# Gate and up projections of 17 of 22 FFN tiles by seven block products, with the down projection between them

## The chip, the cores and the metric

The kernel runs on one core of a Trainium2 chip. The metric is the device time of one execution in microseconds (us), as the median of several runs; less is better.

## What is computed

A trunk of two layers over 512 tokens of width 1024, all in float32. Each layer is a mixer (retention in layer 0, differential attention in layer 1, each with a cross-attention into 256 memory tokens) and a dense feed-forward block. The change touches only the latter:

```python
FFN_DIM = -(-8 * D_MODEL // (3 * 256)) * 256        # 2816
x = x + jnp.concatenate([o_main, o_mem], axis=-1) @ w_out[layer]
h = rms_norm(x, ffn_norm_w[layer])
gu = h @ w_gate_up[layer]
x = x + (jax.nn.silu(gu[..., :FFN_DIM]) * gu[..., FFN_DIM:]) @ w_down[layer]
```

## The kernel before

Activations stand transposed: `xT[0..7]` are eight tiles of 128 features x 512 tokens. TensorE multiplies in float32r, and a float32 product is made of three matmuls: every operand is split into a high half (a rounded copy, made by ACT, `split_h`) and a low half (the rest, a subtraction on DVE, `split_l`), and `mm3` adds high x high, high x low and low x high into one accumulator.

Weights come in chunks of 128 x 1024 (`SPECS`, listed by `chunk_specs`). SP loads a chunk into one of three `wr` pages (`load_chunk`); `split_chunk` makes its halves in one of three `wh` and one of three `wl` pages. `chunk(...)` begins two chunks ahead of use. A page is written again only when its last reader is done, so a load waits for the split of the chunk three before it.

The FFN has 22 feature tiles of 128. `feat_tile` computes one output tile of 128 x 512 into one of eight accumulator banks `ps`, over 8 K tiles of the normed input `xw`. For each feature tile there is a gate and an up product, 2 x 8 x 3 = 48 matmuls of 512 columns. `swiglu` then multiplies both by the token norm `bc` on DVE (they are read from `ps` there), takes Silu on ACT, multiplies on POOL (on DVE for a subset's last tile) and splits the result into `ys` pages (tag `qk`). The 22 tiles go in three subsets (`SUBS`) of 8, 8 and 6; behind each, the down projection of that subset runs for the eight output tiles d, and `add_x` adds each to `xT` on DVE.

What sets the order is `Weave`, at build time. It follows a clock for every engine with costs written in `Engine`, and side streams (generators such as `swiglu` and `split_chunk`) are put into the engines' programs where that clock says that their inputs are ready; `pump` does so after each matmul. On the chip the order on each engine is then fixed: an instruction that waits holds all that stand behind it on its engine.

```python
        for i, (l_, r_) in enumerate(((aH, bH), (aH, bL), (aL, bH))):
            TE.matmul(out, lhsT=l_, rhs=r_, start=start and i == 0, stop=stop and i == 2)
```

Nearly all instructions carry line 251 in the profile (line 283 after the change), which is the helper in `Engine` that records them, so groups are told apart by their tiles.

## Time and profile before

| | us |
|---|---|
| median of 3 runs | 1180.24 |
| lowest and highest | 1178.43, 1182.14 |
| the profiled execution | 1181.2 |
| its span, first to last instruction | 1179.4 |
| PE busy in it | 1166.0 |
| DVE, ACT, POOL busy | 663.7, 480.7, 211.9 |
| one FFN (layer 0), in the span | 359.1 |

The span is read first against the busy time of each engine, then cut into stages. A row's duration runs from an instruction's start to its end; on PE, and by a little on DVE and ACT, neighbours overlap, so a rate is taken from starts.

### The profile page before, as it was taken

How to read it: one execution, taken by the hardware profiler on the slowest of the kernel's cores; microseconds unless marked ns; L12 is line 12 of the kernel's file. 1: busy time of each engine (PE TensorE's matmuls, PEld its weight loads, DVE VectorE, ACT ScalarE, POOL GpSimd, SP SyncE). 2: the span in 40 equal slices, each digit the busy share in tenths (PEclk: the TensorE clock that was granted, in tenths of full speed). 3: DMA queues.
4: the chain of work that ended last, by engine and by line, in shares of the span. 5: the costliest groups of instructions: out<-in, count | busy, mean ns of one | idle time of the engine just before them, and what ended most of it. 6: DMA issues, size and time to landing. Idle time of an engine off the chain costs nothing.

```text
span 1179.4 us, 14244 instructions
## 1 busy us (share of the span) xinstructions
PE 1166.0 (99%) x5546; PEld 966.2 (82%) x5546; DVE 663.7 (56%) x1049; ACT 480.7 (41%) x805; POOL 211.9 (18%) x143
## 2 busy tenths in 40 slices
PE   9999999999999999999999999999999999999998
PEld 7888888888888888888888777888888888888887
DVE  5679894455334443446556688866454344533442
ACT  6566763333213322235455566644332223322321
POOL 4020002211001100001553544224110000100010
PEclk9999999999999999999999999999999999999999
DMA  6432122322322222223422211113223223232322
GB/s 226 137 125 90 66 81 70 106 91 90 107 90 100 97 103 93 89 94 121 143 83 65 104 57 51 47 62 122 89 94 106 91 89 108 90 107 89 101 78 89
DMA packets 35058, 113.26 MB, mean 96 GB/s; under 512 B 4016, under 2 KB 4400, under 8 KB 34992
## 3 DMA queue, kind: packets, MB, share of 16 engines
q1 hardware_dynamic: 34848, 112.34, 27.7%
q8 instruction: 43, 0.70, 0.2%
q14 instruction: 23, 0.19, 0.0%
q10 hardware_dynamic: 144, 0.03, 0.0%
HBM read 110.26 MB, written 2.10 MB: 95 GB/s over the span
## 4 chain that ended last, share of the span: by engine, by line
PE 90%; DVE 5%; ACT 2%; POOL 1%; issue 1%; DMA 0%; SPq 0%; ACTq 0%; DVEq 0%; POOLq 0%
PE ps L251 90%; DVE sm L251 2%; DVE wk L251 2%; POOL tab L251 1%; ACT wk L251 1%; DVE mkL L251 1%; ACT wh L251 0%; DMA wr<-w_t 0%; DVE qk L251 0%; SPq L251 0%; ACT qk L251 0%; ACT L251 0%; ACT xw L251 0%; DVE qc L251 0%; ACT mkY L251 0%
## 5 line engine op out<-in xcount | busy, mean ns | idle before, releaser
L251 PE MATMUL ps<-xw,wh 128*128 128x512 f32 x1624 | 503.1, 390 | 0.0
L251 PEld LDWEIGHTS ps<-xw,wh 128*128 128x128 f32 x1624 | 304.3, 188 | 62.8
L251 ACT ACTIVATE wh<-wr 128x1024 fp32r<-128x1024 f32 (+2 forms) x200 | 204.4, 1024 | 359.9 <-PE ps L251 357.2
L251 DVE TENSOR_TENSOR wl<-wr,wh 128x1024 fp32r<-128x1024 f32 (+2 forms) x177 | 248.1, 1404 | 141.4 <-ACT wh L251 141.2
L251 PE MATMUL ps<-xw,wl 128*128 128x512 f32 x812 | 316.8, 390 | 0.0
L251 PE MATMUL ps<-qk,wh 128*128 128x512 f32 (+1 forms) x836 | 255.3, 386 | 0.0
L251 PEld LDWEIGHTS ps<-qk,wh 128*128 128x128 f32 x836 | 156.2, 188 | 31.8
L251 PEld LDWEIGHTS ps<-xw,wl 128*128 128x128 f32 x812 | 152.5, 188 | 31.0
L251 PE MATMUL ps<-qk,wl 128*128 128x512 f32 (+1 forms) x418 | 161.6, 387 | 0.0
L251 PE MATMUL ps<-wh,xw 128*128 128x512 f32 (+1 forms) x512 | 151.7, 374 | 2.9 <-DVE sm L251 2.9
L251 POOL TENSOR_TENSOR wk<-wk,wk 128x512 f32<-128x512 f32 x38 | 50.4, 1325 | 574.7 <-DVE wk L251 561.2
L251 DVE TENSOR_TENSOR wk<-ps,tab 128x512 f32<-128x512 f32 x94 | 64.4, 687 | 120.4 <-PE ps L251 114.6
L251 DVE TENSOR_TENSOR xT<-ps,xT 128x512 f32<-128x512 f32 (+1 forms) x65 | 44.3, 682 | 152.1 <-PE ps L251 152.0
L251 PEld LDWEIGHTS ps<-wh,xw 128*128 128x128 f32 x512 | 92.6, 191 | 19.2 <-DVE sm L251 3.6
L251 PE MATMUL ps<-wl,xw 128*128 128x512 f32 (+1 forms) x256 | 95.8, 374 | 0.4 <-DVE wl L251 0.4
L251 PEld LDWEIGHTS ps<-qk,wl 128*128 128x128 f32 x418 | 78.5, 188 | 15.6
L251 POOL TENSOR_TENSOR tab<-tab,tab 128x512 f32<-128x512 f32 x31 | 50.8, 1640 | 137.9 <-ACT tab L251 136.9
L251 ACT ACTIVATE qk<-wk 128x512 fp32r<-128x512 f32 (+2 forms) x74 | 41.8, 579 | 66.1 <-POOL wk L251 49.1
L251 POOL TENSOR_TENSOR wl<-wr,wh 128x1024 fp32r<-128x1024 f32 x23 | 55.5, 2417 | 71.8 <-ACT wh L251 67.1
L251 POOL TENSOR_TENSOR sm<-sm,mhalf 128x4 f32<-128x4 f32 (+1 forms) x36 | 44.3, 1238 | 129.0 <-DVE sm L251 128.7
L251 ACT ACTIVATE wk<-wk 128x512 f32<-128x512 f32 x50 | 31.6, 633 | 81.0 <-DVE wk L251 80.9
L251 PEld LDWEIGHTS ps<-wl,xw 128*128 128x128 f32 x256 | 48.8, 191 | 8.4 <-DVE wl L251 0.9
(129 smaller groups left out, 949.4 us busy)
## 6 DMA issues: line engine op xcount, KB each, us to landing
wr<-w_t SPq DMA_DIRECT2D x180, 512.0 KB, 3.5
wr<-w_t SPq DMA_DIRECT2D x16, 384.0 KB, 3.0
wr<-w_t SPq DMA_DIRECT2D x8, 256.0 KB, 5.1
xT<-x_t SPq DMA_DIRECT2D x8, 256.0 KB, 4.9
zo<-mem_t SPq DMA_DIRECT2D x8, 256.0 KB, 4.9
out_t<-xT SPq DMA_DIRECT2D x7, 256.0 KB, 2.0
tab<-dec_t SPq DMA_DIRECT2D x6, 256.0 KB, 3.8
tab<-ali_t SPq DMA_DIRECT2D x6, 256.0 KB, 3.9
```

What stands on the lines that cost most here:

```text
L251: return call(out, *args, **kw)
```

## The change

For the tiles of subset 0 (now 5) nothing changes. For the other 17, gate and up of one feature tile are one matrix product of 2 x 2 blocks: the weights are cut in rows gate and up and in K halves (`a11` gate and `a21` up of K tiles 0 to 3, `a12` and `a22` of K tiles 4 to 7), the input in K halves and in token halves of 256. By the scheme of Strassen in Winograd's form seven products of blocks do in place of eight, each over 4 K tiles, so 4 x 3 = 12 matmuls of 256 columns. For it:

- `token_halves` makes, once a layer while subset 0 runs, four sums of token blocks for each of 4 K tile pairs, split into halves (`tb`, in the pages `v` and `qc`).
- `weight_ops` makes for each tile the four weight sums `s1`, `s2`, `s3`, `s4` on DVE and splits seven operands of 128 x 512. The halves of one operand now share a page; `wh` and `wl` give six such pages, taken in turn, and at most six are live.
- `gate_up_pair` runs the seven products into three accumulators x, z and y. ACT copies x after each of three products and z after one; DVE sums the copies and the rest, applies the norm, and both products of swiglu stand on DVE and ACT.
- The down projection of a subset is cut into two pieces for each d (3 tiles and the rest). These pieces, loaded apart into `wk` pages, stand in the three gaps of each tile of the next subset (after `s1`, `s4`, `a12`); the last subset's run alone at the end.

Subsets are now 5, 6, 5 and 6. The diff's core:

```diff
-SUBS = ((0, 8), (8, 16), (16, 22))
+SUBS = ((0, 5), (5, 11), (11, 16), (16, 22))
+HT = T // 2
+KH = KT // 2
...
+                    if s == 0:
+                        specs.append((("gu", l, f, u), "w_gate_up", l, 0, KT, r(u * FFN + f * P, P)))
+                    else:
+                        both = r(f * P, P) + r(FFN + f * P, P)
+                        specs.append((("st", l, f, u), "w_gate_up", l, u * KH * P, KH, both))
...
-                specs.append((("down", l, s, d), "w_down", l, f0 * P, f1 - f0, r(d * P, P)))
+                for z, (a, b) in enumerate(pieces(s)):
+                    specs.append((("down", l, s, d, z), "w_down", l, (f0 + a) * P, b - a, r(d * P, P)))
...
+def pieces(s):
+    n = SUBS[s][1] - SUBS[s][0]
+    return (0, 3), (3, n)
+def gaps(s):
+    n = 3 * (SUBS[s][1] - SUBS[s][0])
+    skip = max(0, n - 2 * KT)
+    places = [[] for _ in range(n + 1)]
+    for i, z in enumerate((d, z) for d in range(KT) for z in range(2)):
+        places[min(i + skip, n)].append(z)
+    return places
...
+    def token_halves(layer, norm, tb):
+        while KT - 1 not in norm.xw:
+            yield 1.0
+        room = []
+        for tag, n, bufs in (("v", 3, 8), ("qc", KH, 2)):
+            for z in [page(tag, [P, n, HT], bufs, F32R) for _ in range(bufs)]:
+                room += [z[:, i, :] for i in range(n)]
+        a, b = slice(0, HT), slice(HT, T)
+        for j in range(KH):
+            x1, x2 = xT[j], xT[KH + j]
+            w1, w2 = col(norm.c + j), col(norm.c + KH + j)
+            yield from take(wk=3)
+            z = [wk([P, T])[:, s] for _ in range(3) for s in (a, b)]
+            A.activation(z[1], x1[:, b], AF.Copy, scale=w1)
+            V.tensor_tensor(z[0], x1[:, a], x1[:, b], op=ALU.subtract)
+            yield
+            V.scalar_tensor_tensor(z[2], x2[:, b], w2, z[1], op0=ALU.mult, op1=ALU.subtract)
+            V.scalar_tensor_tensor(z[3], x1[:, a], w1, z[2], op0=ALU.mult, op1=ALU.add)
+            V.scalar_tensor_tensor(z[4], x2[:, a], w2, z[3], op0=ALU.mult, op1=ALU.subtract)
+            parts = [(room.pop(), room.pop(), *src) for src in ((z[0], w1), (z[2],), (z[3], -1.0), (z[4], -1.0))]
+            yield
+            for part in parts:
+                yield from split(part)
+            give("wk", 3)
+            tb[j] = [part[:2] for part in parts]
...
+    def weight_ops(layer, order, ops, live):
...
+        def one(key, dH, dL, src, done):
+            W.cur = max(W.ready(src), W.ready(dH) - 0.2)
+            yield
+            split_h(dH, src)
+            yield
+            split_l(dH, dL, src)
+            n = dH.shape[1] // P
+            ops[key] = [[z[:, k * P:(k + 1) * P] for k in range(n)] for z in (dH, dL)]
+            done()
...
+        for key in order:
+            while live[0] >= 6:
+                yield 0.2
+            live[0] += 1
+            if key[0] == "down":
+                while key not in raws:
+                    yield 0.3
+                src = raws[key]
+                def done(key=key):
+                    del raws[key]
+                    give("wk", 1)
+            else:
+                _, _, fk, name = key
+                i1, i2 = [INDEX["st", layer, fk, u] for u in range(2)]
+                while i1 not in loaded or i2 not in loaded:
+                    yield 0.3
+                half = slice(0, T), slice(T, 2 * T)
+                a11, a21, a12, a22 = [loaded[i][0][:, s] for i in (i1, i2) for s in half]
+                if name == "a11":
+                    used1 = last(2, lambda i=i1: load_chunk(i + 3))
+                    used2 = last(3, lambda i=i2: load_chunk(i + 3))
+                    src, done = a11, used1
+                elif name == "s1":
+                    W.cur = max(W.ready(a11), W.ready(a22))
+                    yield
+                    yield from take(wk=2)
+                    s3, s1 = wk([P, T]), wk([P, T])
+                    V.tensor_tensor(s1, a21, a22, op=ALU.add)
+                    V.tensor_tensor(s3, a11, a21, op=ALU.add)
+                    src, done = s1, last(2, lambda: give("wk", 1))
+                    done1 = done
+                elif name == "s2":
+                    yield from take(wk=1)
+                    src = s2 = wk([P, T])
+                    V.tensor_tensor(s2, s1, a11, op=ALU.add)
+                    done1()
+                    used1()
+                    done = done2 = last(2, lambda: give("wk", 1))
+                elif name == "s4":
+                    yield from take(wk=1)
+                    src = wk([P, T])
+                    V.tensor_tensor(src, s2, a12, op=ALU.add)
+                    done2()
+                    used2()
+                    done = lambda: give("wk", 1)
+                elif name == "s3":
+                    src, done = s3, lambda: give("wk", 1)
+                else:
+                    src, done = (a12 if name == "a12" else a22), used2
+            w = page(("wh", "wl")[count % 2], [P, CW], 3, F32R)
+            count += 1
+            n = src.shape[1]
+            W.add(one(key, w[:, :n], w[:, T:T + n], src, done), 0.0)
+            yield 0.1
...
+    def gate_up_pair(layer, fk, norm, tb, ops, live, key, ys, fill):
...
+        def product(name, b, a, first, last):
+            w = ops.at(("st", layer, fk, name))
+            for j in range(KH):
+                act = [z[:, HT * (b - 21):HT * (b - 20)] for z in norm.xw.at(KH + j)] if b in (21, 22) else \
+                    [z[:, lo] for z in norm.xw.at(j)] if b == 11 else tb.at(j)[b]
+                mm3(a[:, lo], (w[0][j], w[1][j]), act, first and j == 0, last and j == KH - 1, True, not first)
+            live[0] -= 1
...
+            V.tensor_tensor(g[:, hi], st["z"][:, lo], part[0][:, hi], op=ALU.add)
...
+            V.tensor_tensor(g[:, lo], st["y"][:, lo], part[0][:, lo], op=ALU.add)
...
+            V.tensor_tensor(g, g, nrm.bc, op=ALU.mult)
+            yield
+            A.activation(g, g, AF.Silu)
...
+            V.scalar_tensor_tensor(u[:, lo], x[:, lo], -1.0, nrm.bc[:, lo], op0=ALU.mult, op1=ALU.mult)
...
+            V.tensor_tensor(part[1][:, hi], part[1][:, lo], part[1][:, hi], op=ALU.add)
+            V.scalar_tensor_tensor(u[:, hi], part[1][:, hi], -1.0, nrm.bc[:, hi], op0=ALU.mult, op1=ALU.mult)
...
+            V.tensor_tensor(u, st["g"], u, op=ALU.mult)
...
+        x = acc()
+        product("a11", 11, x, True, True)
+        A.activation(part[0][:, lo], x[:, lo], AF.Copy)
+        z = acc()
+        product("s1", 0, z, True, True)
+        A.activation(part[1][:, hi], z[:, lo], AF.Copy)
+        fill()
+        product("s2", 2, x, False, True)
+        A.activation(part[0][:, hi], x[:, lo], AF.Copy)
+        product("s4", 22, z, False, True)
+        st["z"] = z
+        W.add(gate())
+        fill()
+        product("s3", 1, x, False, True)
+        A.activation(part[1][:, lo], x[:, lo], AF.Copy)
+        y = acc()
+        product("a12", 21, y, True, True)
+        st["y"] = y
+        fill()
+        product("a22", 3, x, False, True)
+        W.add(up())
...
     def ffn(layer, norm, finished):
+        names = ("a11", "s1", None, "s2", "s4", None, "s3", "a12", None, "a22")
...
+        ops, live, tb, ys = Store(), [2], Store(), [Store() for _ in SUBS]
+        W.add(token_halves(layer, norm, tb), 5.0)
+        for i in range(*SUBS[0]):
+            accs = [acc(), acc()]
+            for u in range(2):
+                w = chunk("gu", layer, i, u)
+                if i == SUBS[0][1] - 1 and u == 1:
+                    W.add(weight_ops(layer, order, ops, live), 0.0)
+                feat_tile(accs[u], w, every(norm.xw, KT))
...
+            for i, fk in enumerate(range(*SUBS[s])):
+                gate_up_pair(layer, fk, norm, tb, ops, live, (s, i), ys[s], fill)
+            fill()
...
+            if d >= KT - 2:
+                begin(after + d - KT + 2)
```

On PE, in layer 0's gate and up stage, one matmul reads 512 tokens. Names are output, then moving and stationary tile; these are the end of a gate product and the start of the up product behind it, before:

```order
L251 MATMUL ps_2401<-xw_2168,wh_2371 128x512
L251 MATMUL ps_2401<-xw_2169,wh_2371 128x512
L251 MATMUL ps_2401<-xw_2168,wl_2372 128x512
L251 MATMUL ps_2472<-xw_1976,wh_2407 128x512
L251 MATMUL ps_2472<-xw_1977,wh_2407 128x512
L251 MATMUL ps_2472<-xw_1976,wl_2408 128x512
```

The same engine in the third tile of subset 1 now: the end of product `s1` (tokens from `v`), then the first down piece of subset 0 (`zo` holds its tiles), 3 tiles in one page:

```order
L283 MATMUL ps_3006<-v_2202,wl_2919 128x256
L283 MATMUL ps_3006<-v_2203,wl_2919 128x256
L283 MATMUL ps_3006<-v_2200,wl_2919 128x256 x3
L283 MATMUL ps_3027<-zo_2347,wh_2934 128x512
L283 MATMUL ps_3027<-zo_2348,wh_2934 128x512
```

The products have become half as wide and the down projection has moved from behind a subset to between the products of the next.

On DVE, one tile of the gate and up stage before, from its gate read to its second weight split:

```order
L251 TENSOR_TENSOR wk_2475<-ps_2400,tab_2252 128x512
L251 TENSOR_TENSOR wk_2476<-ps_2401,tab_2252 128x512
L251 TENSOR_TENSOR wl_2480<-wr_2381,wh_2479 128x1024
L251 TENSOR_TENSOR qk_2498<-wk_2476,qk_2497 128x512
L251 TENSOR_TENSOR wl_2516<-wr_2419,wh_2515 128x1024
```

DVE now, about half a tile of subset 1: weight sums (`wk<-wr`, `wk<-wk,wr`), low halves (`wl<-wk,wl`, `wh<-wk,wh`), an add into `xT`, and the reads of y and x:

```order
L283 TENSOR_TENSOR wk_2915<-wr_2724 128x512
L283 TENSOR_TENSOR wl_2919<-wk_2916,wl_2919 128x512
L283 TENSOR_TENSOR wk_2949<-wk_2916,wr_2724 128x512
L283 TENSOR_TENSOR wh_2934<-wk_2776,wh_2934 128x384
L283 TENSOR_TENSOR xT_81<-ps_2895,xT_81 128x512
L283 TENSOR_TENSOR wk_2965<-wk_2949,wr_2770 128x512
L283 TENSOR_TENSOR wl_2953<-wk_2949,wl_2953 128x512
L283 TENSOR_TENSOR wk_2898<-ps_2932,wk_2805 128x256
L283 TENSOR_TENSOR wk_2898<-wk_2898,tab_2300 128x512
L283 SCALAR_TENSOR_TENSOR wk_2988<-ps_2807,tab_2300 128x256
L283 TENSOR_TENSOR wk_2806<-wk_2806 128x256
L283 SCALAR_TENSOR_TENSOR wk_2988<-wk_2806,tab_2300 128x256
```

Weight sums, more and shorter splits and the reads of three accumulators have moved between one another on DVE.

DVE at the end of layer 0's FFN before, the last tile's swiglu and the first down output:

```order
L251 TENSOR_TENSOR wk_4282<-ps_4208,tab_2252 128x512
L251 TENSOR_TENSOR wk_4283<-ps_4209,tab_2252 128x512
L251 TENSOR_TENSOR wk_4283<-wk_4282,wk_4283 128x512
L251 TENSOR_TENSOR wl_4287<-wr_4189,wh_4286 128x768
L251 TENSOR_TENSOR qk_4302<-wk_4283,qk_4301 128x512
L251 TENSOR_TENSOR xT_80<-ps_4280,xT_80 128x512
```

DVE at the same place now (`ps_5524` is x of the last tile, ready with its last product):

```order
L283 TENSOR_TENSOR wk_5616<-wk_5616,tab_2300 128x512
L283 SCALAR_TENSOR_TENSOR wk_5700<-ps_5524,tab_2300 128x256
L283 TENSOR_TENSOR wk_5523<-wk_5523 128x256
L283 SCALAR_TENSOR_TENSOR wk_5700<-wk_5523,tab_2300 128x256
L283 TENSOR_TENSOR wl_5679<-wk_5662,wl_5679 128x384
L283 TENSOR_TENSOR wk_5700<-wk_5616,wk_5700 128x512
L283 TENSOR_TENSOR wh_5699<-wk_5671,wh_5699 128x384
L283 TENSOR_TENSOR qk_5730<-wk_5700,qk_5729 128x512
L283 TENSOR_TENSOR xT_80<-ps_5697,xT_80 128x512
```

Between the last product and the last tile's split two sums more and two down splits have moved in.

## Rows read from the trace of the kernel before

**Rows 1.** The page: busy time by engine, and the span in 40 slices.

```profile
span 1179.4 us, 14244 instructions
PE 1166.0 (99%) x5546; PEld 966.2 (82%) x5546; DVE 663.7 (56%) x1049; ACT 480.7 (41%) x805; POOL 211.9 (18%) x143
PEclk9999999999999999999999999999999999999999
```

**Rows 2.** Chain that ended last, two longest pieces: start us, us, what.

```profile
127.90 468.20 PE ps L251 x2157
820.30 355.81 PE ps L251 x1589
```

**Rows 3.** Stretches, columns as headed: FFN of layer 0; its first gate and up stage.

```profile
core 0: us, PE busy (x) PEld busy (x) DVE busy (x) ACT busy (x) POOL busy (x), PEclk, DMA share, GB/s
214.50:573.60 359.10, 359.10 (x1590) 297.37 (x1589) 170.39 (x187) 110.45 (x137) 36.96 (x27) 1.00 0.29 99
214.50:301.50 87.00, 87.00 (x389) 72.08 (x388) 43.11 (x50) 27.56 (x34) 11.78 (x9) 1.00 0.28 97
```

**Rows 4.** 512 columns in layer 0's FFN: timeline of PE; then its stretch.

```profile
324.00 0.62 PE L251 MATMUL ps<-qk,wh 128*128 128x512 f32 x2
...
329.44 0.62 PE L251 MATMUL ps<-qk,wh 128*128 128x512 f32 x2
324.00:330.00 6.00, 6.00 (x28) 4.98 (x27) 2.30 (x4) 1.42 (x2) 0.00 (x0) 1.00 0.24 87
```

**Rows 5.** 256 columns in layer 1's query projection: timeline of PE; then its stretch.

```profile
585.70 0.41 PE L251 MATMUL ps<-wh,xw 128*128 128x256 f32 x2
...
593.26 0.40 PE L251 MATMUL ps<-wh,xw 128*128 128x256 f32 x2
585.70:593.26 7.56, 7.56 (x65) 7.56 (x64) 5.16 (x12) 2.61 (x6) 6.75 (x6) 1.00 0.49 175
```

**Rows 6.** Timeline of DVE at the end of subset 0, layer 0.

```profile
302.56 0.69 DVE L251 TENSOR_TENSOR wk<-wk,wk 128x512 f32<-128x512 f32 x1
303.17 1.22 DVE L251 TENSOR_TENSOR wl<-wr,wh 128x1024 fp32r<-128x1024 f32 x1
```

**Rows 7.** Groups by shape: count, then busy us and mean ns, then idle before.

```profile
L251 DVE TENSOR_TENSOR wk<-ps,sm 128x256 f32<-128x256 f32 x12 | 5.0, 420 | 2.0 <-POOL sm L251 1.9
L251 DVE SCALAR_TENSOR_TENSOR v<-zo,par,v 128x256 fp32r<-128x256 f32 x8 | 3.3, 477 | 0.0
L251 DVE TENSOR_TENSOR wk<-ps,wk 128x384 fp32r<-128x384 f32 x9 | 5.0, 551 | 1.2 <-ACT wk L251 1.0
L251 ACT ACTIVATE qk<-wk 128x512 fp32r<-128x512 f32 x56 | 35.4, 633 | 65.8 <-POOL wk L251 49.1 <-DVE wk L251 16.5
L251 ACT ACTIVATE wk<-ps 128x256 f32<-128x256 f32 x6 | 2.3, 383 | 3.5 <-PE ps L251 3.5
```

**Rows 8.** Timeline of DVE and POOL in subset 0, layer 0; idle in brackets.

```profile
258.24 0.69 DVE L251 TENSOR_TENSOR wk<-ps,tab 128x512 f32<-128x512 f32 x1 [2.70 <-PE ps L251]
259.08 1.29 POOL L251 TENSOR_TENSOR wk<-wk,wk 128x512 f32<-128x512 f32 x1 [9.60 <-DVE wk L251]
259.16 2.29 DVE L251 TENSOR_TENSOR wl<-wr,wh 128x1024 fp32r<-128x1024 f32 x1 [0.23 <-ACT wh L251]
```

**Rows 9.** Timeline at the last subset's end, layer 0.

```profile
540.92 0.62 PE L251 MATMUL ps<-qk,wh 128*128 128x512 f32 x2
541.12 0.69 DVE L251 TENSOR_TENSOR wk<-ps,tab 128x512 f32<-128x512 f32 x1 [3.18 <-PE ps L251]
...
542.64 0.64 ACT L251 ACTIVATE qk<-wk 128x512 fp32r<-128x512 f32 x1 [0.85 <-DVE wk L251]
543.40 0.68 DVE L251 TENSOR_TENSOR qk<-wk,qk 128x512 fp32r<-128x512 f32 x1
```

**Rows 10.** DMA issues: count, KB each, us to landing.

```profile
wr<-w_t SPq DMA_DIRECT2D x16, 384.0 KB, 3.0
```

**Rows 11.** Groups by shape in layer 0's FFN: weight loads, mean ns of one.

```profile
L251 PEld LDWEIGHTS ps<-xw,wh 128*128 128x128 f32 x699 | 131.2, 188 | 27.4
```

More of the change, by code (lines that the diff above doesn't have):

```diff
@@ L436, in load_chunk @@
     def load_chunk(i):
-        if i in loaded or i >= len(SPECS):
+        if i in loaded or i >= RING:
             return
@@ L452, in begin @@
     def begin(i):
-        if i not in begun and i < len(SPECS):
+        if i not in begun and i < RING and SPECS[i][0][0] != "st":
             begun.add(i)
@@ L1295, in swiglu @@
         yield
-        yH, yL = qk([P, T]), qk([P, T])
+        o = zo if key < 3 else qk
+        yH, yL = o([P, T], F32R), o([P, T], F32R)
         yield from split((yH, yL, gu[1]))
@@ new lines, in weight_ops, with pieces_in, last, used @@
+    def weight_ops(layer, order, ops, live):
+        count, raws, sums = 0, {}, {}
+        def pieces_in():
+            for key in order:
+                if key[0] == "down":
+                    while len(raws) >= 3:
+                        yield 0.3
+                    yield from take(wk=1)
+                    i = INDEX[key]
+                    n = SPECS[i][4] * P
+                    raws[key] = wk([P, T])[:, :n]
+                    DMA.dma_start(raws[key], w_d[i][:, :n])
+        W.add(pieces_in())
+        def one(key, dH, dL, src, done):
[7 more added lines that the diff above has]
+            done()
+        def last(n, then):
+            left_ = [n]
+            def used():
+                left_[0] -= 1
+                if left_[0] == 0:
+                    then()
+            return used
+        for key in order:
+            while live[0] >= 6:
+                yield 0.2
+            live[0] += 1
+            if key[0] == "down":
+                while key not in raws:
[8 more added lines that the diff above has]
+                while i1 not in loaded or i2 not in loaded:
+                    yield 0.3
+                half = slice(0, T), slice(T, 2 * T)
[21 more added lines that the diff above has]
+                elif name == "s4":
+                    yield from take(wk=1)
+                    src = wk([P, T])
[12 more added lines that the diff above has]
+            yield 0.1
@@ new lines, in ffn, with down, fill @@
+    def ffn(layer, norm, finished):
+        names = ("a11", "s1", None, "s2", "s4", None, "s3", "a12", None, "a22")
+        order = []
+        for s in range(1, len(SUBS) + 1):
+            if s < len(SUBS):
+                places = iter(gaps(s))
+                for fk in range(*SUBS[s]):
+                    for n_ in names:
+                        order += [("st", layer, fk, n_)] if n_ else [("down", layer, s - 1, *p) for p in next(places)]
+                order += [("down", layer, s - 1, *p) for p in next(places)]
+            else:
+                order += [("down", layer, s - 1, d, z) for d in range(KT) for z in range(2)]
+        ops, live, tb, ys = Store(), [2], Store(), [Store() for _ in SUBS]
[7 more added lines that the diff above has]
+                feat_tile(accs[u], w, every(norm.xw, KT))
+            W.add(swiglu(accs, norm.nrm, i, ys[0], G))
+        live[0] -= 2
+        downs = {}
+        def down(s, d, z):
+            if z == 0:
+                downs[d] = acc()
+            a, b = pieces(s)[z]
+            w = ops.at(("down", layer, s, d, z))
+            feat_tile(downs[d], w, [(k - a, ys[s], k) for k in range(a, b)], z == 0, z == 1)
+            live[0] -= 1
+            if z == 1:
+                add_x(d, downs[d])
+        for s in range(1, len(SUBS)):
+            places = iter(gaps(s))
+            def fill():
+                for p in next(places):
+                    down(s - 1, *p)
+            for i, fk in enumerate(range(*SUBS[s])):
+                gate_up_pair(layer, fk, norm, tb, ops, live, (s, i), ys[s], fill)
+            fill()
+        s = len(SUBS) - 1
+        after = INDEX["st", layer, FFN // P - 1, 1] + 1
+        for d in range(KT):
+            if d >= KT - 2:
+                begin(after + d - KT + 2)
+            if (layer, d) == (DEPTH - 1, KT - 1):
+                for cols in (slice(0, T // 2), slice(T // 2, T)):
+                    o = acc()
+                    for z, (a, b) in enumerate(pieces(s)):
+                        w = ops.at(("down", layer, s, d, z))
+                        feat_tile(o, w, [(k - a, ys[s], k) for k in range(a, b)], z == 0, z == 1, cols)
+                    add_x(d, o, cols)
+                    finished(d, cols)
+                continue
+            for z in range(2):
+                down(s, d, z)
+            if d == 0:
+                give("tab", 1)
+            finished(d)
```

70 lines of the change are left out of this document (44 added, 26 removed).

## The prediction

> **What bounds the kernel now.** I read the shares of the span first: PE is busy for 1166.0 of 1179.4 us and its granted clock stands at nine tenths or more, the 2.4 GHz level, in all 40 slices; no other engine passes 56% [rows 1]. Then the chain that ended last: its two longest pieces are PE alone, 468.20 us from 127.90 and 355.81 us from 820.30 [rows 2]. Both feed-forward blocks (FFN) lie in them; layer 1's is the second piece. The table by stretches gives layer 0's FFN: 359.10 us, PE busy in all of it at clock 1.00, DVE in 170.39, ACT in 110.45 [rows 3]. So there a matmul less is worth its whole step, as long as the other engines can still feed PE.
>
> A busy PE row overlaps its neighbours, so I take the step between starts. 512 columns: 24 matmuls lie between the starts 324.00 and 329.44, that is 5.44 / 24 = 0.2267 us [rows 4]. The FFN checks it: 22 feature tiles x 48 gate and up matmuls plus 528 down matmuls are 1584, x 0.2267 = 359.1 us [rows 3].
>
> **PE's gain.** In 17 of 22 tiles a layer the 48 matmuls of 512 columns (2 outputs x 8 K tiles x 3 float32r terms) become 7 products x 4 K tiles x 3 terms = 84 matmuls of 256. The order shows 1632 of the long ones gone and 2856 short ones there. The columns fall by an eighth; the time falls less, since a short one costs more than half a long one. The trace has that shape in layer 1's query projection: 63 matmuls lie between the starts 585.70 and 593.26, so 7.56 / 63 = 0.120 us, each with its own weight load [rows 5]. A tile was 48 x 0.2267 = 10.88 us and becomes 84 x 0.120 = 10.08; 0.80 us x 34 tiles = **27.2 us**. The down projection keeps its 528 matmuls of 512 a layer; only its place changes.
>
> In that projection PEld is busy for 7.56 of 7.56 us, against 4.98 of 6.00 us under 512 columns [rows 4, 5]. The Trainium skill, Perfetto Trace Analysis, section Identifying the Most-Contended Engine, says that TensorE's headroom is to be read from the busy share of weight loads and not of matmuls. By that the short products would be at a limit that the long ones had not reached, and nothing more would come from narrower ones. The sum by the measured step already holds that limit, so I keep 0.120.
>
> **What DVE and ACT must do for it.** A row's mean holds some 0.08 us that overlaps the next instruction: the 0.69 us multiply at 302.56 is followed at 303.17, so 512 elements cost 0.61 [rows 6]. From the rows by shape [rows 7], less 0.08: 256 elements 0.34 (0.40 with a column scalar), 384 elements 0.47; on ACT 512 0.55, 256 from PSUM 0.30, 384 about 0.40 between them. Per block tile the order has on DVE 4 weight sums, 7 low halves, 2 multiplies and one output split of 512 (14 x 0.61), 3 sums of 256 (1.02) and 2 scaled ones (0.80): 10.36 us. In the stretch of 17 tiles there are also 24 adds into xT (14.6) and 48 splits of down pieces (32 x 0.47 + 16 x 0.34 = 20.5): 17 x 10.36 + 35.1 = 211 us. PE needs there 17 x 10.08 plus the down projection of the first 16 tiles (384 x 0.2267 = 87.0), 258 us. DVE is thus loaded to 82%, from under half [rows 3]. ACT: 17 x (9 x 0.55 + 4 x 0.30) + some 18 = 123 us, 48%. POOL loses 28 products of swiglu, and with them the wait that made a 1.22 us low half last 2.29 beside it [rows 8]; that wait was hidden and buys nothing on PE.
>
> All this I cost at nothing, hidden under PE. The cover is the six pages of split weights: two in use, four ready, each good for 1.36 to 2.04 us of PE, 5 to 8 us in all. Making one takes 0.55 on ACT, 0.61 on DVE and two handovers of about 0.2 [rows 8, 9], some 1.6 us. Walking the DVE and ACT rows by these steps over the first two block tiles, low halves come 3 to 6 us before their product. If the cover were gone, each late page would cost up to 1.6 us.
>
> The first 5 tiles hide the token sums: 4 x (2 x 0.34 + 6 x 0.40) = 12.3 us on DVE, which is busy for 43.11 of 87.0 us in such a stage [rows 3], so 27 + 12 of 54.4. SP starts 64 down loads a layer in place of 24, queued between the loads of gate and up blocks; the bytes stay. 384 KB land in 3.0 us [rows 10] and a piece has 192 at most; three are asked for ahead and one lasts 2.04 us on PE, so 6.1 us cover 3.0 + 0.9.
>
> **Two seams cost something.** At a layer's end the last tile's output must be ready when PE, past its last product, has run five of six tiles of the first down output: 5 x 0.68 = 3.40 us, 3.63 for the low half. Before, that chain (multiply, silu product, split) ran from 540.92 to 544.08 [rows 9]. Now it is 0.20 + 0.40 + 0.34 + 0.40 for the three sums, 0.47 for a down split that stands between, 0.69 multiply, 0.67 ACT with its handover, 0.15, 0.69, 0.20 = 4.2 us: PE waits **0.6 us**. The bounds are 0 (an earlier wait has put PE behind by as much) and 1.5 (one more ACT and DVE row in the way). At the first tile of subsets 1 and 3 no down piece stands between products, so ACT must read the accumulator within one product, 12 x 0.120 = 1.44 us: 0.20 + 0.38 + 0.20, and 0.63 more behind one split [rows 7], is 1.41. With a second row ahead PE waits 0.55; I take **0.5 us** a layer, bounds 0 and 1.1. No mechanism lets these seams fall below nothing: PE has no wait there now.
>
> **Sum.** 1179.4 - 27.2 + 2 x (0.6 + 0.5) = 1154.4 us of span. The profiled execution took 1181.2, its span is 1.8 shorter, and the median of the runs, 1180.24, lies 0.84 above that span: **1155.2 us**. Without seams 1153.0; with both at their ends (2 x 2.6) 1158.2.
>
> **Rivals.** *Late weights.* DVE stands still at each read of an accumulator with the next weight halves behind it in its queue. If one 0.61 us operation a block tile comes out from under PE, 34 x 0.61 = 20.7 us go back: 1173.7; half of that, 1163. For it: 82% load in a fixed order. Against: 3 to 6 us of reserve.
>
> *DVE becomes the bound, slower than before.* Per block tile with its share of down work DVE needs 211 / 17 = 12.4 us, PE 15.2; before, it was 10.88 + 5.12 = 16.0. DVE may idle 2.8 us a tile for nothing; from 3.6 the change loses. Today it idles 2.70 us at one such read [rows 8]. If two of these stood in every tile, in a circle with PE waiting for weights, a tile takes 17.8: 1180.2 + 34 x 1.8 = 1241. For it: five reads of accumulators a tile on DVE, four on ACT. Against: today's wait is slack, it ends when PE has finished, and PE never waits for it [rows 3].
>
> *The load shows.* If a short matmul were paced by the 0.188 us that a load row lasts [rows 11], a tile takes 84 x 0.188 = 15.8 us, 4.9 more: 1347. The Trainium skill, TensorE: Matmul & The Clock Gate, section The mechanism, says that a weight load overlaps running matmuls only for other row groups of the array, and these loads fill all rows; by that rule it would go this way. Against it: 0.120 us over 63 in a row, and 0.2267 for 512 columns, with full loads in both [rows 4, 5].
>
> **How the numbers follow.** Forecast 0.80 (1152 to 1160). Late weights 0.10 (1160 to 1176.7). A loss of about all the gain 0.03. DVE as the bound 0.06, the load 0.01. A measurement tells 0.3%, 3.5 us, from no change. Faster 0.90, same 0.03, slower 0.07. Range 1151.5 (no seam, and the runs' lower half) to 1165: it leaves out the slower cases, the loss, and part of the late weights, under 0.2.
>
> **What would show it.** Right: starts 0.120 us apart within a product, each FFN near 346.6 us, DVE busy some 80% of the block stretch, PE's waits under 2 us a layer and at the seams. Wrong: waits of PE for wh or wl all through the stretch (late weights), DVE without gaps (its bound), steps above 0.13 us (load).

## The result and the profile after

The changed kernel takes **1152.07 us** (median of three runs, 1150.44 to 1154.38; a fourth took 4084.89 us, far outside the rest, and is left out) beside 1179.34 for the kernel before on the same chip. The ratio is 0.977, 95% interval 0.974 to 0.980. Beside the later experiments it was run again: 1151.03 us, 0.975 (0.973 to 0.976). The forecast was 1155.2 in a range of 1151.5 to 1165.

First the page of the changed kernel, with the lines of [rows 1]:

```profile
span 1148.7 us, 18021 instructions
PE 1134.8 (99%) x6770; PEld 995.6 (87%) x6770; DVE 881.9 (77%) x1679; ACT 608.9 (53%) x1231; POOL 172.8 (15%) x115
PEclk9999999999999999999999999999999999999999
```

PE is still the engine that is never free. DVE went from 56% to 77% of the span and PE did not notice. The span is 30.7 us shorter, and the profiled execution is 1150.44 us. The chain that ended last (start us, us, what) has in its two longest pieces again nothing but PE, as in [rows 2], but each FFN now breaks once, at its end:

```profile
127.46 396.26 PE ps L283 x2469
...
529.60 51.73 PE ps L283 x272
...
803.93 306.03 PE ps L283 x2027
...
1115.84 29.56 PE ps L283 x146
```

The table by stretches is read as [rows 3] was: first layer 0's FFN, then in it the 17 block tiles.

```profile
core 0: us, PE busy (x) PEld busy (x) DVE busy (x) ACT busy (x) POOL busy (x), PEclk, DMA share, GB/s
214.05:558.79 344.74, 344.16 (x2202) 312.61 (x2201) 281.59 (x502) 174.21 (x350) 16.56 (x13) 1.00 0.33 103
268.45:528.02 259.57, 259.57 (x1827) 243.13 (x1826) 214.58 (x393) 131.38 (x271) 1.29 (x1) 1.00 0.34 109
```

344.74 us stand where 359.10 stood, 14.36 less. In the block stretch PE is busy in every hundredth, DVE in 83% of it, ACT in 51%. The steps are read from a timeline of PE (start us, us, operation, count) inside a tile:

```profile
296.50 0.52 PE L283 MATMUL ps<-qc,wl 128*128 128x256 f32 x3
296.86 1.18 PE L283 MATMUL ps<-v,wl 128*128 128x256 f32 x9
297.88 2.22 PE L283 MATMUL ps<-zo,wh 128*128 128x512 f32 x9
299.93 0.52 PE L283 MATMUL ps<-qc,wl 128*128 128x256 f32 x3
300.29 1.22 PE L283 MATMUL ps<-v,wl 128*128 128x256 f32 x9
301.35 1.59 PE L283 MATMUL ps<-xw,wh 128*128 128x256 f32 x12
302.78 1.55 PE L283 MATMUL ps<-qk,wl 128*128 128x512 f32 x6
304.17 0.52 PE L283 MATMUL ps<-qc,wh 128*128 128x256 f32 x3
```

A product is 12 matmuls of 256 columns. s1, on a token sum (pages qc and v), runs from 296.50 to 297.88: 1.38 us, 0.115 each, and 0.113 in its last nine (1.02 / 9). s2, also on a sum, runs from 299.93 to 301.35: 1.42, 0.118 each. s4, on xw, from 301.35 to 302.78: 1.43, 0.119 each. A down piece of six matmuls of 512 columns takes 302.78 to 304.17, 1.39 us, 0.232 each, where [rows 4] had 0.2267. That down step is slow only at its start: over all pieces between products the first three matmuls of a piece behind s1 step at 231 to 232 ns on average, the first five behind s4 or a12 at 228 to 236, and those after them at 226.7. These differences were not in the forecast; four of the experiments are on the short steps.

Last, the end of the layer, as [rows 9] showed it before: the timeline there.

```profile
524.95 2.20 PE L283 MATMUL ps<-qk,wl 128*128 128x512 f32 x9
...
525.26 0.69 DVE L283 TENSOR_TENSOR wk<-wk,tab 128x512 f32<-128x512 f32 x1
525.88 0.42 DVE L283 SCALAR_TENSOR_TENSOR wk<-ps,tab 128x256 f32<-128x256 f32 x1
...
528.19 0.63 ACT L283 ACTIVATE qk<-wk 128x512 fp32r<-128x512 f32 x1 [1.15 <-DVE wk L283]
...
528.85 0.69 DVE L283 TENSOR_TENSOR qk<-wk,qk 128x512 fp32r<-128x512 f32 x1 [0.23 <-ACT qk L283]
528.87 0.50 PE L283 MATMUL ps<-qk,wh 128*128 128x512 f32 x1 [0.36 <-ACT qk L283]
...
529.60 0.74 PE L283 MATMUL ps<-qk,wh 128*128 128x512 f32 x2 [0.22 <-DVE qk L283]
```

The last product ends where the down matmuls start, at 524.95; its accumulator is first read at 525.88, behind two operations of the gate half on DVE, the second of them the multiply at 525.26. The last tile's high half comes from ACT at 528.82, PE starts at 528.87; the low half from DVE at 529.54, PE starts at 529.60. The last matmul before the first gap starts 0.75 us before 528.87, the next gap lasts 0.73 from start to start; less a step of 0.23 each, PE loses 1.0 us a layer. There are no other new waits of PE in its list.

### The profile page after: what moved, and what is told of

The parts are those of the page before. It is cut to its first block, busy times and chain, and to the rows that moved or that the text cites. A ratio compares the mean times of both kernels' runs of the same rounds, so it can differ in the third digit from the quotient of the medians.

```text
span 1148.7 us, 18021 instructions
## 1 busy us (share of the span) xinstructions
PE 1134.8 (99%) x6770; PEld 995.6 (87%) x6770; DVE 881.9 (77%) x1679; ACT 608.9 (53%) x1231; POOL 172.8 (15%) x115
## 4 chain that ended last, share of the span: by engine, by line
PE 89%; DVE 6%; ACT 3%; POOL 1%; issue 1%; DMA 0%; SPq 0%; DVEq 0%; ACTq 0%; POOLq 0%
PE ps L283 89%; DVE wk L283 2%; DVE sm L283 2%; POOL tab L283 1%; ACT wk L283 1%; DVE mkL L283 1%; ACT wh L283 1%; DVE qk L283 0%; DMA wr<-w_t 0%; ACT qk L283 0%; ACT xw L283 0%; ACT L283 0%; SPq L283 0%; DVE qc L283 0%; ACT mkY L283 0%
## 5 line engine op out<-in xcount | busy, mean ns | idle before, releaser
L283 PE MATMUL ps<-xw,wh 128*128 128x256 f32 (+1 forms) x1208 | 257.6, 331 | 0.0
L283 PEld LDWEIGHTS ps<-xw,wh 128*128 128x128 f32 x1208 | 184.3, 189 | 20.2
L283 PE MATMUL ps<-xw,wl 128*128 128x256 f32 (+1 forms) x820 | 178.5, 318 | 0.0
L283 ACT ACTIVATE wk<-ps 128x256 f32<-128x256 f32 (+4 forms) x198 | 84.6, 430 | 169.1 <-PE ps L283 168.2
L283 PE MATMUL ps<-qk,wh 128*128 128x512 f32 (+1 forms) x567 | 148.0, 388 | 1.2 <-ACT qk L283 0.7
L283 ACT ACTIVATE wh<-wr 128x1024 fp32r<-128x1024 f32 (+1 forms) x130 | 113.5, 877 | 29.7 <-PE ps L283 23.4
L283 DVE TENSOR_TENSOR wh<-wk,wh 128x384 fp32r<-128x384 f32 (+2 forms) x138 | 83.2, 603 | 33.6 <-ACT wh L283 33.4
L283 DVE TENSOR_TENSOR wl<-wk,wl 128x512 fp32r<-128x512 f32 (+2 forms) x126 | 78.4, 622 | 35.3 <-ACT wl L283 35.0
L283 PE MATMUL ps<-v,wl 128*128 128x256 f32 x702 | 94.3, 279 | 0.0
L283 ACT ACTIVATE wl<-wk 128x512 fp32r<-128x512 f32 (+2 forms) x126 | 71.0, 563 | 39.8 <-DVE wk L283 26.3
L283 PEld LDWEIGHTS ps<-v,wl 128*128 128x128 f32 x702 | 87.5, 189 | 0.0
```

Source lines behind the costliest of these rows:

```text
L283: return call(out, *args, **kw)
```

## The experiments

Times are medians; each ratio is to the kernel before on the same chip, with its 95% interval. The changed kernel stands at 0.975 to 0.977.

```
kernel       us        ratio (95%)              what it is
e_order      1181.20   1.000  (0.999 - 1.001)   new order, ordinary tiles
e_noweave    1148.25   0.972  (0.971 - 0.973)   block products, down not between them
e_dve3       1149.46   0.973  (0.972 - 0.975)   three low halves a tile made twice
e_dve7       1229.21   1.041  (1.039 - 1.043)   seven
e_tail       1148.85   0.972  (0.969 - 0.975)   layer end in another order
e_swap       1151.90   one run                  operands exchanged
e_same       1150.72   one run                  equal values in all sums
e_fill       1146.15   0.970  (0.969 - 0.972)   down pieces at other places in the tile
e_align      1161.09   0.983  (0.981 - 0.985)   other addresses, same instructions
e_best19     1141.84   0.967  (0.965 - 0.968)   e_fill + e_tail + 19 block tiles
e_best20     1155.86   0.979  (0.977 - 0.980)   the same with 20
after_again  1151.03   0.975  (0.973 - 0.976)   the changed kernel
```

**Is it the columns? (e_order)** The core of the edit: four half-K weight pages, no sums, 48 matmuls of 512 columns.

```
-        names = ("a11", "s1", None, "s2", "s4", None, "s3", "a12", None, "a22")
+        names = ("a11", None, "a12", None, "a21", None, "a22")
...
+            feat_tile(accs[-1], w, [(k, norm.xw, h + k) for k in range(KH)], h == 0, h > 0)
```

> Undoes the block products alone: the 17 tiles are ordinary ones again (48 matmuls of 512 columns, weights split as four half-K pages a tile without sums), with the down projection of one subset between the parts of the next one's tiles, the same subsets and the same pages. Theory (the gain is the columns of PE and nothing else): the gain is gone, both FFN near 359 to 361 us, the time 1179 to 1182 us, ratio to the kernel before 1.000 +- 0.003. Rival (the new order or the smaller subsets save or cost time by themselves): under 1176 or over 1184.

1181.20 us, ratio 1.000. The stretch of layer 0's FFN in its trace:

```profile
215.00:574.31 359.31, 359.14 (x1588) 297.22 (x1587) 183.06 (x297) 129.81 (x232) 44.05 (x30) 1.00 0.30 99
```

359.31 us against 359.10 of [rows 3]: order, pieces and smaller subsets by themselves give and cost nothing. All of the gain is the block products'.

**Does the weaving hide DVE? (e_noweave)**

```
-        places[min(i + skip, n)].append(z)
+        places[n].append(z)
```

> Undoes the second part of the change alone: the down projection of a subset stands in one piece behind the next subset's block products, not between them. Theory (the weaving is what hides DVE): within the products alone PE takes 9.7 to 9.9 us a tile and DVE needs 10.4 and its waits, so DVE is the bound there; the pages of split weights cover a few us a subset; PE waits for wh or wl, 0.5 to 1 us a tile for 34 tiles, 12 to 34 us: 1164 to 1186. Rival (six pages are cover enough, the place of the down pieces does not matter): 1147 to 1155, no rows of waits for wh or wl. By theory D of the step, s1, s2, s3 and a22 all step every 113 ns here, since no 512-column matmul stands between the products.

1148.25 us: the theory fell. Not 12 to 34 us were lost; the time is some 3 us below the changed kernel's, on another chip and with the intervals of the two ratios just overlapping. PE's waits (total us, times, longest) and the stretch of the six tiles of subset 1:

```profile
PE ps L283 <- DVE wl L283: 2.9, 5, 0.9
PE ps L283 <- DVE wh L283: 0.7, 2, 0.4
268.85:328.89 60.04, 59.10 (x506) 58.69 (x504) 56.37 (x104) 37.17 (x76) 1.29 (x1) 1.00 0.33 98
```

DVE is busy for 56.4 of 60.0 us there, nearly as long as PE, so the ready pages shrink slowly; the first wait falls in the fifth of the six tiles, and after the sixth comes a whole down projection in which the pages fill up again. What the theory missed is that the shortage starts anew with each subset: by the trace every subset has one wait, of 0.3 to 0.9 us, each in its fifth tile, 3.2 us in both layers (the list's other 0.4 lies near 6.8 us, where the kernel before waits too). Against them stand the layer ends, which no longer wait, and faster steps (the sums 113 ns, the down matmuls 226.8 ns on average, as no long matmul stands between the products). So the second half of the change is not what carries the first.

**Where does DVE begin to count? (e_dve3, e_dve7)**

In e_dve3 (e_dve7 has all seven names in the condition):

```
             split_l(dH, dL, src)
+            if key[0] == "st" and key[3] in ("a11", "s2", "s3"):
+                split_l(dH, dL, src)
```

> Doubles a suspected cost: the low half of three of a tile's seven split pages is computed twice, 3 x 0.61 = 1.8 us more of DVE a tile, 31 us a layer. DVE's share of the 264 us stretch of the 17 tiles goes from 82% (217.6 us) to 94%. Theory (DVE's work is hidden as long as it is less than PE's): within 4 us of the changed kernel, 1152 to 1156. Rival (late weights: what is added to DVE comes out from under PE since it follows a fixed order): up to 3 x 0.61 x 34 = 62 us, 1170 to 1214, with PE's waits for wh and wl in every tile.

> The same for all seven pages: 7 x 0.61 = 4.3 us more of DVE a tile, 73 us a layer, so DVE would need 217.6 + 72.6 = 290 us where PE has 264. Theory (DVE is the bound from the point where its work fills PE's time): at least 26 us a layer longer, 1204, and with DVE's waits for accumulators (some 10% of the stretch) up to 1240; PE waits for wh and wl in every tile, DVE busy over 95% of the stretch. Rival (more room than the sums say): under 1190.

The 264 us stretch of the block tiles in e_dve3, then the same tiles in e_dve7, and two rows of e_dve7's waits of PE:

```profile
265.10:529.10 264.00, 263.64 (x1845) 246.22 (x1843) 248.35 (x450) 134.62 (x276) 1.29 (x1) 1.00 0.35 110
265.30:569.10 303.80, 277.36 (x1845) 254.20 (x1843) 294.00 (x517) 131.58 (x276) 1.29 (x1) 0.97 0.30 94
PE ps L283 <- DVE wl L283: 30.0, 20, 2.7
PE ps L283 <- DVE wh L283: 20.9, 16, 2.7
```

The only wait of DVE for PE that the list of e_dve7's stretch has (total us, times, longest):

```profile
DVE xT L283 <- PE ps L283: 1.4, 1, 1.4
```

With 31 us more on DVE a layer it is busy for 248.35 of 264.00 us, 94%, and the stretch and the time stay (1149.46). With 76 us more it needs 294.0, PE waits for wl and wh, and the stretch is 303.8: 39.8 us longer, twice that 79.6, close to the 77 us of the time. DVE is then idle for 9.8 us in 17 tiles, 0.6 us a tile. The bound by DVE exists, then. A load of 94% of PE's time costs nothing and one of 111% (294.0 on 264.0) does; where between them it sets in, no run tells. The change stands at 83%.

**The layer's end (e_tail)**

```
-                order += [("down", layer, s - 1, d, z) for d in range(KT) for z in range(2)]
+                first = [(0, 0), (1, 0), (0, 1), (1, 1)]
+                order += [("down", layer, s - 1, *p) for p in first + [(d, z) for d in range(2, KT) for z in range(2)]]
```

> The wait at a layer's end, two of about 0.5 us a layer in the changed kernel (ACT qk and DVE qk). Here the first down piece of the second output stands ahead of the last piece of the first output, so PE has 2.04 us more of work before it needs the last tile. Theory (PE waits for the last tile's output chain): both waits vanish, 1.0 us a layer, time 1150.0 to 1150.5 us against some 1152 for the changed kernel. Rival (what ends late is the chain's share of ACT and DVE behind the down splits, and grows with a split more ahead): the waits stay or move to the pieces' weights wh, time 1152 or more.

1148.85 us, and the rows ACT qk and DVE qk are gone from PE's waits. The stretch of the FFN:

```profile
214.76:558.31 343.55, 343.55 (x2202) 312.68 (x2201) 280.99 (x502) 174.37 (x350) 16.49 (x13) 1.00 0.33 103
```

343.55 against 344.74: 1.2 us a layer, with PE busy in all of it. The wait was the last tile's chain and nothing took its place.

**What sets the short step? (e_swap, e_same, e_fill, e_align)** First the exchange of operands, the second argument of each product (11, 21 and 22 are xw, 0 to 3 the sums):

```
-        product("a11", 11, x, True, True)
+        product("a11", 3, x, True, True)
...
-        product("s1", 0, z, True, True)
+        product("s1", 2, z, True, True)
...
-        product("s2", 2, x, False, True)
+        product("s2", 0, x, False, True)
...
-        product("s4", 22, z, False, True)
+        product("s4", 11, z, False, True)
...
-        product("s3", 1, x, False, True)
+        product("s3", 22, x, False, True)
...
-        product("a22", 3, x, False, True)
+        product("a22", 1, x, False, True)
```

Then, in e_same, equal values in all four sums:

```
-            parts = [(room.pop(), room.pop(), *src) for src in ((z[0], w1), (z[2],), (z[3], -1.0), (z[4], -1.0))]
+            parts = [(room.pop(), room.pop(), *src) for src in ((z[0], w1),) * 4]
```

> Why the 256-column step is 120, 118 or 113 ns. In the changed kernel products a11, s4 and a12 (moving operand xw) step every 120 ns, s2, s3 and a22 (sums 2, 1 and 3) every 117.6, s1 (sum 0) every 113. Here the moving operands change places: a11 reads sum 3, s1 sum 2, s2 sum 0, s4 the first half of xw, s3 the second half, a22 sum 1 (so the output is not the reference's). Theory A, the step goes with what is read as moving operand: s2 113, a11, s1 and a22 117.6, s4, s3 and a12 120. Theory B, it goes with the place of the product (its weights, its position in the tile): each product keeps its step, a11 120, s1 113. Theory C, a sum on a freshly started bank: a11 and s1 113, s2 and a22 117.6, s4, s3 and a12 120. The time is about 1152 us by all three (1150 by C).

> Of theory A two kinds: the values of the moving operand or its place in SBUF. All four token sums of a K tile get the values of sum 0 here, each in its own pages as before (so the output is not the reference's). If the values decide: s1, s2, s3 and a22 all step every 113 ns, 84 matmuls a tile then take 36 x 0.120 + 48 x 0.113 = 9.74 us in place of 9.90, and the time falls by 34 x 0.16 = 5.4 us to about 1147. If the place decides: 117.6 stays for s2, s3 and a22, and the time stays at 1152.

Neither A nor B nor C held in full. The steps, as medians of the later matmuls of each product over its 34 occurrences (ns, from start to start):

```
product   after      e_swap     e_same     e_fill     e_align
a11       120 xw     118 sum    120 xw     120 xw     120 xw
s1        113 sum    118 sum    113 sum    113 sum    120 sum
s2        118 sum    118 sum    118 sum    113 sum    120 sum
s4        120 xw     120 xw     120 xw     120 xw     120 xw
s3        118 sum    120 xw     118 sum    113 sum    120 sum
a12       120 xw     120 xw     120 xw     120 xw     120 xw
a22       118 sum    118 sum    118 sum    113 sum    120 sum
down 512 (mean)  229.5   -      -          228.5      233.6
```

In e_same nothing moves: the values have no part in it. In e_swap 120 goes with xw and 118 with the sums whatever product reads them (theory A), but s2 with sum 0 does not step at 113:

```profile
300.08 0.52 PE L283 MATMUL ps<-qc,wl 128*128 128x256 f32 x3
300.43 1.22 PE L283 MATMUL ps<-v,wl 128*128 128x256 f32 x9
301.49 1.59 PE L283 MATMUL ps<-xw,wh 128*128 128x256 f32 x12
```

From 300.08 to 301.49 that is 1.41 us, 0.1175 each. No sum product stood directly behind a short product on xw in e_swap, and 113 was nowhere. So e_fill puts all four there:

```
-        names = ("a11", "s1", None, "s2", "s4", None, "s3", "a12", None, "a22")
+        names = ("a11", "s1", "s2", None, "s4", "s3", None, "a12", "a22", None)
```

> The rows of the two runs on the step leave a fourth theory (D): the step depends on what ran before. A product on a token sum steps every 113 ns where it stands directly behind a 256-column product on xw, and every 117.6 where a 512-column down piece, or only other sums behind one, stand ahead of it (with the operands exchanged none stood behind xw, and 113 was gone). Here the down pieces move within the tile: a11, s1, s2, piece, s4, s3, piece, a12, a22, piece, so that all four sum products follow xw directly; the matmuls are the same. D: s1, s2, s3 and a22 step every 113 to 115 ns, 36 matmuls a tile save some 4 ns, 34 x 36 x 0.0042 = 5 us: about 1147 against 1152 of the changed kernel. Rival (113 belongs to s1 alone): s2, s3 and a22 stay at 117.6, time 1152. Second rival: the accumulator of a11 must now be read within one product (1.4 us), and PE waits for ACT there; 0.2 to 0.5 us x 34 = 7 to 17 us slower, 1159 to 1169.

1146.15 us. Its timeline, s4 and s3 of one tile:

```profile
305.78 1.60 PE L283 MATMUL ps<-xw,wl 128*128 128x256 f32 x12
307.22 0.52 PE L283 MATMUL ps<-qc,wh 128*128 128x256 f32 x3
307.57 1.18 PE L283 MATMUL ps<-v,wh 128*128 128x256 f32 x9
308.60 2.22 PE L283 MATMUL ps<-zo,wl 128*128 128x512 f32 x9
```

s3 now runs from 307.22 to 308.60, 1.38 us where it took 1.41: theory D held for s1, s2, s3 and a22, and no accumulator was read late. That leaves why xw and the sums differ. They lie in different places: by the addresses that the program gives them, the pages of xw and of the split weights start at 768 B modulo 1024, those of the sums at 448. e_align changes the layout alone, so that all of these start at 448:

```
+    for tag, n, bufs in (("wh", CW, 3), ("wl", CW, 3), ("xw", T, 2 * KT)):
+        page(tag, [P, n], bufs, F32R)
     warm = small(1)
```

> Where in SBUF the operands lie, as a cause of the step. By the addresses of the changed kernel the pages of split weights and of xw begin at 768 B modulo 1024 and those of the token sums at 448; the products on xw step every 120 ns, those on sums 113 to 118. Here the same instructions run with three pools of pages laid out in another order, so that weights, xw and sums all begin at 448 modulo 1024 (down's moving operands stay at 768). Theory E (the place of the moving operand itself decides): xw's products step every 113 to 118 too, 36 matmuls x 34 tiles x 2 to 6 ns = 2.5 to 7 us less, 1145 to 1149. Theory F (the place relative to the weights decides, equal is slow): the sums' products step every 120 as xw's do, 48 x 34 x 3 ns = 5 us more, 1156. Rival (neither, the place has no part in it): every step as it was, 1151 to 1153.

1161.09 us, and every short matmul steps at 120, the sums' too. Its timeline: an ordinary tile, where xw and weights lie alike, then s2, s4 and two down pieces of one block tile:

```profile
239.61 0.62 PE L283 MATMUL ps<-xw,wh 128*128 128x512 f32 x2
...
245.73 0.62 PE L283 MATMUL ps<-xw,wh 128*128 128x512 f32 x2
...
304.54 1.57 PE L283 MATMUL ps<-qk,wl 128*128 128x512 f32 x6
305.95 0.52 PE L283 MATMUL ps<-qc,wh 128*128 128x256 f32 x3
...
307.38 1.60 PE L283 MATMUL ps<-xw,wl 128*128 128x256 f32 x12
308.82 2.27 PE L283 MATMUL ps<-zo,wh 128*128 128x512 f32 x9
310.93 0.52 PE L283 MATMUL ps<-qc,wl 128*128 128x256 f32 x3
```

s4 takes 1.44 us from 307.38, exactly 0.120 each; the nine long matmuls take 308.82 to 310.93, 0.234 each. What theory F forecast for the steps came: the sums did not move modulo 1024, the weights did, and the sums' step went from 113 or 118 to 120. Its 1156 us had left the long matmuls out. They behave the other way round, which was not expected: the down projection's operands stayed at 768 while the weights moved to 448, and its step rose to 233.6 ns. The weights' new place by itself is not the cause there, as the ordinary tile tells: with xw at 448 too, 27 matmuls of 512 columns lie between the starts 239.61 and 245.73, 0.2267 each, as before. In these runs short matmuls were faster with unlike places, long ones with like places. The sum fits: 17 x 2 x (10.08 - 9.90) = 6.1, 768 x 4.1 ns = 3.1, and some 1 us in the last down projections, 10 us against the measured 9 to 10. Why it is so, and which bits of the address count, these runs don't tell. For the short ones unlike places were seen in one pair alone, operand at 448 and weights at 768; xw at unlike places was not tried.

The Trainium skill, TensorE: Matmul & The Clock Gate, section Step-by-step: what each phase is for, says that loading the next weights takes no SBUF read bandwidth from the running matmul, since both have ports of their own. No run here measures that directly. With the same instructions the step went from 113 or 118 to 120 ns when the layout alone changed, so it depends on where the two operands lie; whether their two reads get in each other's way is not shown.

**Put together (e_best19, e_best20, after_again)** e_fill's and e_tail's edits, and

```
-SUBS = ((0, 5), (5, 11), (11, 16), (16, 22))
+SUBS = ((0, 3), (3, 8), (8, 13), (13, 18), (18, 22))
```

in e_best19, ((0, 2), (2, 7), (7, 12), (12, 17), (17, 22)) in e_best20, with pages zo for the odd subsets in place of the even ones, and the first subset's down pieces cut at 2 of its 3 tiles (at 1 of 2 in e_best20).

> The changed kernel itself, beside the two versions of this call on one chip: 1150 to 1153 us, PE's gaps of about 0.73 us twice at each layer's end.

> What the runs point to, put together: the down pieces behind a22, s2 and s3 (5.6 us), the first piece of the second output ahead at the layer's end (2 us), and 19 block tiles a layer in place of 17, in five subsets of 3, 5, 5, 5 and 4 tiles: each further block tile replaces 48 x 0.2267 = 10.88 us by 84 matmuls that take 9.77, 1.11 us, 4 of them 4.4. Theory (PE's columns and seams alone count, DVE is hidden up to 94% of PE): 1152 - 5.6 - 2 - 4.4 = 1140. Rival (more splits and adds of down pieces, 16 and 8 a layer more, or the shorter first subset bring weights late): waits for wl or wh behind the first block tiles, 1143 or more.

> The same with 20 block tiles, subsets of 2, 5, 5, 5 and 5: 1137.8 us by the theory. The first subset is only 2 tiles, 21.8 us, in which DVE must make 12.3 us of token sums, two swiglu tiles (4 us with their splits) and the first weights. Rival: the token sums or weights of the first block tile come late once a layer, 1 to 5 us each, or down pieces of one tile wait for its output: 1140 to 1148.

e_best19 takes 1141.84 us, 0.967 of the kernel before, 9.2 us below the changed kernel beside it; 12 were expected. In its FFNs PE waits once, 1.0 us, for a low half in layer 0's last down projection; the other 2 us that are missing are not explained. e_best20 takes 1155.86. The mechanism of its rival showed, late token sums, but the time lies far above the rival's 1140 to 1148. Its waits of PE, the timeline at the first block tile, and a stretch of low clock there:

```profile
PE ps L284 <- ACT v L284: 9.7, 4, 4.1
PE ps L284 <- DVE v L284: 2.1, 4, 0.7
244.53 1.44 ACT L284 ACTIVATE v<-wk 128x256 fp32r<-128x256 f32 x3
244.68 0.58 PE L284 MATMUL ps<-v,wl 128*128 128x256 f32 x1 [4.09 <-ACT v L284]
243.04:249.87 6.83, 4.48 (x17) 4.09 (x18) 3.81 (x10) 2.85 (x8) 0.00 (x0) 0.50 0.00 0
```

PE stands 4.09 us in the middle of s1 until ACT has made the next token sum. The waits are 11.8 us in both layers. In the middle of the longest one the granted clock falls to 0.50, the 1.2 GHz level, for 6.83 us, and PE's 4.48 us of matmuls run in it at half the pace; the same stands in layer 1 with 3.94. That is some 4 us more, which the rival had not counted. Two ordinary tiles, 21.8 us, are not enough cover for the sums; three were.

## Why the prediction was right, point by point

**What bounds it** held: matmuls off PE's path came off the time, in e_order they came back.

**The step of 0.120 us** was right for products on xw and too long for those on sums. The 1428 short steps of a layer sum to 168.4 us, not 171.4; a tile took 9.90 us, not 10.08. The step was taken from one place [rows 5] whose operands lay like xw here; e_align, where all lie so, gives 0.120 everywhere. 3.0 us a layer more gain.

**Down unchanged at 0.2267** was the small miss in the other direction: between short products its matmuls average 229.5 ns (228.5 behind s1, 230.1 behind s4 and a12), 384 x 2.8 ns = 1.1 us a layer. In e_noweave, where they stand together, they average 226.8.

**DVE and ACT at nothing** held. 82% was worked out for DVE and 48% for ACT, 83% and 51% are there; the row of 94% in e_dve3 shows how far DVE could have gone. The reason given, six pages as a reserve, is borne out by e_noweave, where they carried four tiles of a subset without help. A down piece of 192 KB landed in 3.7 us, not under the 3.0 taken for it, and no row of PE waits for it.

**The seam at the layer's end**: the mechanism was right (e_tail), the size was not, 1.0 for 0.6 us, within its bounds. The chain had left out that two operations of the gate half stand ahead on DVE when the last product ends: it reads the accumulator 0.93 us later, not 0.20, and ends at 4.6 us (524.95 to 529.54), not 4.2.

**The seam at the first tiles** cost nothing for 0.5: the timeline has no gap of PE there, and in e_fill each tile reads an accumulator within one product without a wait.

**The sum.** 1154.4 was forecast for the span, 1148.7 came. Steps 2 x -3.0, down 2 x +1.1, layer ends 2 x +0.4, first tiles 2 x -0.5: -4.0. The other 1.7 fits a difference between two executions: the profile of before has two stretches of 3.4 us at 1.2 GHz in layer 1's mixer, that of the changed kernel one (last section). Misses of both signs met in the sum, 7.0 us one way and 3.0 the other, so part of its closeness is luck.

**The rivals.** *Late weights*: no wait of PE for wh or wl in the block stretch. (Its 1173.7 was counted from the sum without seams; with them it is 1175.9.) *DVE as the bound*: real, but its price was argued wrongly. It took the 2.70 us that DVE stands today at an accumulator [rows 8] as idle time that would stay in a circle with PE; in e_dve7, where PE did wait for weights, DVE idled 0.6 us a tile and waited for PE once in the stretch, 1.4 us: a late DVE found its accumulators finished. From what load it decides is thus told by DVE's work, not by its waits.

*The load shows*: no, the steps are 0.113 to 0.120 us and not 0.188. The Trainium skill's rule on row groups (TensorE: Matmul & The Clock Gate, section The mechanism), taken alone, would have given the latter. The Trainium skill's other rule, that headroom is to be read from weight loads (Perfetto Trace Analysis, section Identifying the Most-Contended Engine), agrees in part: PEld is busy for 243.13 of 259.57 us in the block stretch, and yet e_fill took another 2.3 us a layer out of it with the same loads.

## What to carry to other kernels

Where PE alone is the path, cost a change by columns at the measured step, and look whether the other engines' work, not their waits, stays under PE's time; here a load of 94% still cost nothing. Work that runs ahead through a few pages needs its cover only until the next stretch that lets the pages fill up, so count a shortage per stretch and not per program. And take a matmul's step from a place where both operands lie as they will lie: up to 6% hung on the layout here.

## What the runs showed of the hardware

A 256-column float32r matmul with a weight load of its own stepped at 113, 118 or 120 ns, a 512-column one at 226.7 to 233.6, at a granted clock of 1.00. The step depended on the layout of moving operand and weights in SBUF. The short matmuls with unlike places also depended on what ran before: 113 behind a short product of like places, 118 behind a long one. The long ones with like places were slower in the first three to five behind a short product, 228 to 236, and then 226.7.

Some waits of PE cost more than themselves. In the kernel before, PE starts one matmul at 602.41 and the next at 604.94; from 605.94 on the granted clock is 0.50 (1.2 GHz) for 3.4 us. The changed kernel has the same gap twice over, 2.52 us from 587.63 in its first profile and 2.53 from 588.09 in the second, and only the second profile shows the drop. The rows are two of the kernel before, then one of each profile behind that gap:

```profile
602.41:604.94 2.53, 0.39 (x3) 0.03 (x1) 2.28 (x4) 0.40 (x1) 2.53 (x2) 1.00 0.00 0
605.94:609.34 3.40, 3.40 (x10) 2.66 (x9) 1.39 (x3) 1.47 (x2) 3.40 (x3) 0.50 0.72 259
590.20:593.61 3.41, 3.41 (x16) 2.83 (x17) 1.39 (x3) 2.00 (x3) 3.41 (x3) 1.00 0.68 184
590.90:594.31 3.41, 3.41 (x11) 2.64 (x10) 1.39 (x3) 2.00 (x3) 3.15 (x3) 0.50 0.67 190
```

PE is busy in all of the low stretch, so about half of its 3.4 us, 1.7, is lost on top of the gap. In the profiles here such drops stood behind or in gaps between PE's starts of 2.1 to 4.4 us, not behind each of them, and none behind the gaps of 0.7 us at a layer's end. Times of one kernel differ by such amounts: the runs of the changed kernel with mean clocks of 0.999, 0.997 and 0.996 took 1150.44, 1152.07 and 1154.38 us. In e_dve7 PE's waits for wl and wh, 50.9 us, are less than the 77 us lost; PE was also busy for 277.36 us a stretch against 263.64 in e_dve3, at a mean clock of 0.97. DVE set the time there, so it is not shown that the low clock cost anything by itself.
